# A decoder layer with 32 experts on one core: the split of an expert's fourth weight strip, ahead of the condition or behind it

## The chip, the cores and the metric

The kernel runs on one core of a Trainium2 chip. The core has TensorE (PE in the rows; its weight loads are PEld), VectorE (DVE), ScalarE (ACT), GpSimd (POOL) and SyncE (SP), which work at the same time and wait for one another through semaphores, and 16 DMA engines that all queues share. The metric is the device time of one execution in microseconds (us), lower is better. Three runs of the kernel before took 1853.65, 1854.08 and 1859.51 us; the median is 1854.08 us.

## What is computed

One decoder layer over 2048 tokens of width 1024, all in float32. A first sublayer mixes along the sequence (a state-space branch and a convolution branch, gates, an output projection, LayerNorm). The second sublayer is a mixture of 32 experts: each token goes to two experts of one group, and an expert's rows are worked off in blocks of 128:

```python
def expert_block(args):
    idx, e = args
    xb = xt[idx]
    hid = jax.nn.silu(xb @ w_gate[e]) * (xb @ w_up[e])
    return hid @ w_down[e]
```

The weighted results are summed back to their tokens, and a last LayerNorm follows. `w_gate[e]` and `w_up[e]` are 1024 x 256, `w_down[e]` is 256 x 1024. 4096 assignments over 32 experts make 128 rows an expert on average, so that an expert has one block of rows, or two, or three; the kernel reads the counts at run time.

## The kernel before

The change lies in the loop over the experts (`for e in range(NE)`, lines 1520 to 1552), which is written out 32 times. Order on each engine is the order in which the code is written; an engine works its queue off in that order, and an instruction that waits holds up all that is behind it.

**Weights.** An expert's weights come in as float32 and are split into a high part (a copy rounded to a shorter format, by ACT) and a low part (what is left, a subtraction by DVE), so that three matmuls with the short format stand for one in float32. The raw weights lie in `RAW[i]` (rows: `eraw`) for gate and up, side by side, and in `RD` (`erd`) for down; the split ones in `GU[i]` (`egu`) and `DN[i]` (`edn`). There are two sets, `i` = 0 and 1, for even and odd experts. Gate-and-up is cut into four strips, k = 0 to 3, of 256 rows each, and down into two, k = 4 and 5. `high(i, k)` is the copy on ACT (L1245), `low(i, k)` the subtraction on DVE, `step(i, k)` one after the other. The subtraction of a strip also sets its part of `RAW` free: `load(e, i)` has four DMAs on SP's queue, two (gate and up, L1223 and L1224) for strips 0 and 1 and two for strips 2 and 3, each of 512 KB; `load2` has one of 1 MB for down (L1229).

**A pass for expert e** (j = e % 2) does the matmuls of e, and splits the weights of e + 1 beside it:

1. POOL gathers the rows of the next expert into `XN` and, in conditions on the count (L1527), those of the second and third block of e into `X1` and `X2` (rows: `xhi`, `xlo`).
2. `step(1 - j, 0, 1, 2)` and `high(1 - j, 3)`: three strips of e + 1, and the copy of the fourth.
3. `block(e, 0, j)`: `gateup`, 24 matmuls of 128x512 into `pg`, three for each of 8 pieces of 128 rows of the weights, then `act`: SiLU on ACT and the product on DVE (`hid`).
4. `low(1 - j, 3)`, and `load(e + 3, 1 - j)`.
5. `turn(XN[j])`: 8 transposes of the next expert's rows on PE into `pt`, then the high part by ACT and the low part by DVE into the one tile `B` (`bhl`), which the next `gateup` reads. The third matmul of a `gateup` is the first that reads a low part of `bhl`.
6. `down(1 - j)`: 12 matmuls into `pd`, the down projection of the previous expert's last block.
7. `further(e, 1)`: a condition on the count (L1486). Where the expert has a second block, its body turns `hid` (`turnh`, 2 transposes into `ph`), emits the block before (`emit_last`: two copies of `pd` into `yy` by ACT, scaled by `ll`, with the split of `ph` into `hh` and `hl` in between, and a scatter with addition into `acc` by POOL, L1465), and does the second block with `gateup`, `act`, `turn(X1)` and `down`; a third block is nested in it. Else the body is `turnh` alone.
8. `emit(LQ ...)`: the same emission with the factor `lq`, of whichever block is due, with the split of `ph` (`hh` on ACT, L1447, `hl` on DVE) in between.
9. The two strips of down, k = 4 and 5, and `load2(e + 3, 1 - j)`.

Items 2, 4 and 9 stand only for `more`, that is for e = 1 to 30. PE, ACT, DVE and POOL all take the branch of L1486; SP has no condition there. `yy` has two buffers.

The lines of items 2 to 5 in the loop:

```python
        if more:
            step(1 - j, 0, 1, 2)
            high(1 - j, 3)
        block(e, 0, j, GU[j])
        if more:
            low(1 - j, 3)
            if e + 3 < NE:
                load(e + 3, 1 - j)
        turn(XN[j])
```

Of the kernel before, what the change touches and what calls it, by code (L numbers as in the profile page):

```python
# [26 lines left out]
NE = 32  # L27
# [58 lines left out]
def layer(ctx, tc, a, out, dbg=None):  # L86
# [17 lines left out]
    def bigt(shape, dt, name):  # L104
        n = 1
        for d in shape[1:]:
            n *= d
        return big.tile(shape, dt, name=name, tag="big", bufs=NBIG)
# [1107 lines left out]
    def rows(w, e):  # L1216
        return (w[e] if isinstance(e, int) else w[ds(e, 1)][0]).rearrange("(k p) f -> p k f", p=128)

    def load(e, i, halves=(0, 1)):
        if RAW[i] is None:  # L1220
            RAW[i] = bigt([128, 8, 512], F32, f"eraw{i}")
        for h in halves:
            SP.dma_start(RAW[i][:, 4 * h:4 * h + 4, 0:256], rows(wg, e)[:, 4 * h:4 * h + 4])  # L1223
            SP.dma_start(RAW[i][:, 4 * h:4 * h + 4, 256:512], rows(wu, e)[:, 4 * h:4 * h + 4])  # L1224

    def load2(e, i, q=SP):
        if not RD:
            RD.append(bigt([128, 2, 2, D], F32, "erd"))
        q.dma_start(RD[0][:, i], rows(wd, e))  # L1229


    def parts(i, k):
        if k < 4:
            if GU[i][k // 2] is None:
                GU[i][k // 2] = bigt([128, 2, 4, 512], F32R, f"egu{i}{k // 2}")
            t, r = GU[i][k // 2], k % 2
            return t[:, 0, 2 * r:2 * r + 2, :], t[:, 1, 2 * r:2 * r + 2, :], RAW[i][:, 2 * k:2 * k + 2, :]
        if DN[i] is None:
            DN[i] = bigt([128, 2, 2, D], F32R, f"edn{i}")
        return DN[i][:, 0, k - 4, :], DN[i][:, 1, k - 4, :], RD[0][:, i, k - 4, :]  # L1240

    def high(i, *ks):
        for k in ks:
            h, l, src = parts(i, k)
            A.activation(h, src, AF.Copy)  # L1245

    def low(i, *ks):
        for k in ks:
            h, l, src = parts(i, k)
            V.tensor_tensor(l, src, h.bitcast(F32), op=OP.subtract)  # L1250

    def step(i, *ks):
        for k in ks:
            high(i, k)
            low(i, k)
# [153 lines left out]
    def table(e):  # L1409
        CNT[e] = nc.values_load(cnt[0:1, e:e + 1], engines=ENG, min_val=0, max_val=S)  # L1410

    def gather(xb, idx):
        G.indirect_dma_start(out=xb, out_offset=None, in_=hd,
                             in_offset=bass.IndirectOffsetOnAxis(ap=idx, axis=0),
                             bounds_check=S - 1, oob_is_err=False)
# [6 lines left out]
    def turn(xb):  # L1422
        for b in range(2):
            for k in range(4):
                PE.transpose(PT[b][:, k, :], xb[:, (4 * b + k) * 128:(4 * b + k + 1) * 128], ident)
            hi = B[:, 4 * b:4 * b + 4, 0]
            A.activation(hi, PT[b], AF.Copy)
            V.tensor_tensor(B[:, 4 * b:4 * b + 4, 1], PT[b], hi.bitcast(F32), op=OP.subtract)
# [13 lines left out]
    def turnh():  # L1442
        for k in range(2):
            PE.transpose(PH[:, k, :], HID[:, 128 * k:128 * k + 128], ident)

    def splith():
        A.activation(HH, PH, AF.Copy)  # L1447
        V.tensor_tensor(HL, PH, HH.bitcast(F32), op=OP.subtract)

    def down(j):  # L1450
        dn = DN[j]
        for h in range(2):
            c = slice(512 * h, 512 * h + 512)
            for k in range(2):
                PE.matmul(PD[h], HH[:, k, :], dn[:, 0, k, c], start=k == 0, stop=False)
                PE.matmul(PD[h], HH[:, k, :], dn[:, 1, k, c], start=False, stop=False)
                PE.matmul(PD[h], HL[:, k, :], dn[:, 0, k, c], start=False, stop=k == 1)

    def emit(idx, factor, between=None):
        y = ep.tile([128, D], F32, name="yy", bufs=2)  # L1460
        for h in range(2):
            A.activation(y[:, 512 * h:512 * h + 512], PD[h], AF.Copy, scale=factor.bitcast(F32))  # L1462
            if not h and between:
                between()
        G.indirect_dma_start(out=acc, out_offset=bass.IndirectOffsetOnAxis(ap=idx, axis=0),  # L1465
                             in_=y, in_offset=None, bounds_check=S - 1, oob_is_err=False, compute_op=OP.add)

    def emit_last(e, between=None):
        emit(LL[:, e, 0:1], LL[:, e, 1:2], between)

    def block(e, b, i, gu):

        gateup(i, gu)
        act(i)

    def further(e, b):


        j = e % 2

        def end(b):
            turnh()
            if b > 1 and not e:
                emit(TAB[:, e, b - 2, 0:1], TAB[:, e, b - 2, 1:2])

        with tc.If(CNT[e] > 128 * b) as c:  # L1486
            end(b)
            if b > 1 and e:
                emit(TAB[:, e, b - 2, 0:1], TAB[:, e, b - 2, 1:2], splith)
            elif b == 1 and e:  # L1490
                emit_last(e - 1, splith)
            else:
                splith()
            block(e, b, (e + b) % 2, GU[j])
            if e + 1 < NE or b + 1 < JB:
                turn(XB[b])
            down(j)
            if b + 1 < JB:
                further(e, b + 1)
            else:  # L1500
                end(b + 1)
        with c.Else():
            end(b)
# [16 lines left out]
    for e in range(NE):  # L1520
        j = e % 2
        more = 0 < e < NE - 1
        if e + 2 < NE:
            table(e + 2)
        if e + 1 < NE:
            gather(XN[1 - j], NX[:, e + 1, 0:1])
        with tc.If(CNT[e] > 128):  # L1527
            gather(X1, NX[:, e, 1:2])
            if JB > 2:
                with tc.If(CNT[e] > 256):  # L1530
                    gather(X2, NX[:, e, 2:3])
        if more:
            step(1 - j, 0, 1, 2)
            high(1 - j, 3)
        block(e, 0, j, GU[j])
        if more:
            low(1 - j, 3)
            if e + 3 < NE:
                load(e + 3, 1 - j)
        turn(XN[j])  # L1540
        if e:
            down(1 - j)
        further(e, 1)
        if e:
            emit(LQ[:, e, 0:1], LQ[:, e, 1:2], splith)
        else:
            splith()
        if more:
            high(1 - j, 4, 5)
            low(1 - j, 4, 5)  # L1550
            if e + 3 < NE:
                load2(e + 3, 1 - j)
# [162 lines left out]
```

## Time and profile before

| what | value |
|---|---|
| median of three runs | 1854.08 us |
| the profiled execution, its own time | 1854.43 us |
| its span, first to last instruction | 1852.7 us |
| mean granted TensorE clock | 0.968 of full speed |
| TensorE busy with matmuls | 1703.9 us (92%) |
| VectorE busy | 1317.4 us (71%) |
| ScalarE busy | 692.4 us (37%) |

The span holds 1852.7 us of the execution's 1854.43 us; 1.7 us lie around it. A timeline row gives start and length in us, engine, line, operation, tiles (out<-in), shape and count; a bracket behind it is the time that the engine stood idle before it, and what it had waited for. L66 is the line of a helper through which all PE and DVE instructions go, so these are told apart by their tiles. "DVEq" is DVE's sequencer, here at the branch of L1486. The matmuls of a group overlap: the 24 of a `gateup` follow one another every 0.23 us, though a single one is shown with some 0.4 us.

### The profile page before, as it was taken

The numbers are of one execution on the slowest core, as the hardware profiler recorded it, in microseconds if no ns is written. First come the engines' busy times: TensorE is split into PE (matmuls) and PEld (weight loads), VectorE is DVE, ScalarE is ACT, GpSimd is POOL, SyncE is SP. The second block draws the span as 40 slices with busy tenths as digits, with TensorE's granted clock in tenths as the row PEclk, the third lists the DMA queues.
The fourth block names the chain that finished last, engine by engine and source line by source line (L and its number), as shares of the span: only waits on it lengthen the run. The fifth ranks groups of instructions, "written<-read, shape, count | busy, mean of one in ns | idle before, by whom it ended". The sixth has DMA issues, their size and how long they took to land. (4 is left out here: it accounts for less than half of the span.)

```text
span 1852.7 us, 23925 instructions
## 1 busy us (share of the span) xinstructions
PE 1703.9 (92%) x8368; PEld 1371.0 (74%) x8369; DVE 1317.4 (71%) x2429; ACT 692.4 (37%) x1069; POOL 312.6 (17%) x319
## 2 busy tenths in 40 slices
PE   8999999999999999999999999973999999999930
PEld 7888877777777778777888888862777787777730
DVE  5798787777876874766576778885675556657648
ACT  5111221222222222633321122324675556666744
POOL 2000001101110101000000012212343233333315
PEclk9999999999999999999999999986999999999975
DMA  6321432432342336333463423546988878789755
GB/s 215 95 92 46 119 78 71 145 98 77 100 149 70 101 99 222 109 122 114 172 191 119 148 92 115 182 164 197 304 266 256 253 211 253 230 261 327 223 176 231
DMA packets 214027, 300.81 MB, mean 162 GB/s; under 512 B 29391, under 2 KB 159521, under 8 KB 211313
## 3 DMA queue, kind: packets, MB, share of 16 engines
q1 hardware_dynamic: 166496, 213.32, 35.0%
q0 software_dynamic: 23152, 56.06, 11.6%
q10 hardware_dynamic: 24224, 29.47, 4.8%
q8 instruction: 86, 1.41, 0.3%
q14 instruction: 69, 0.56, 0.1%
HBM read 224.77 MB, written 92.31 MB: 171 GB/s over the span
## 5 line engine op out<-in xcount | busy, mean ns | idle before, releaser
L66 PE MATMUL mm<-xh,whi 128*128 128x512 f32 x896 | 360.8, 403 | 0.0
L66 PE MATMUL mm<-xl,whi 128*128 128x512 f32 x896 | 353.6, 395 | 0.0
L66 PE MATMUL mm<-xh,wlo 128*128 128x512 f32 x896 | 352.1, 393 | 0.0
L66 PE MATMUL pg<-egu,bhl 128*128 128x512 f32 x1176 | 287.4, 399 | 25.1 <-DVEq L1486 20.7
L66 DVE SCALAR_TENSOR_TENSOR cvw<-cvw,cw 128x1024 f32<-128x1024 f32 x240 | 292.1, 1280 | 0.0
L66 PEld LDWEIGHTS pg<-egu,bhl 128*128 128x128 f32 x1176 | 217.9, 189 | 78.1 <-issue 14.2
L66 PEld LDWEIGHTS mm<-xh,whi 128*128 128x128 f32 x896 | 168.3, 188 | 47.9 <-ACT y L712 5.8
L66 PEld LDWEIGHTS mm<-xh,wlo 128*128 128x128 f32 x896 | 168.2, 188 | 41.6
L66 PEld LDWEIGHTS mm<-xl,whi 128*128 128x128 f32 x896 | 168.6, 188 | 36.5 <-DVE xl L66 0.3
L66 PE MATMUL mm<-yt,whi 128*128 128x512 f32 x512 | 163.7, 401 | 2.0 <-ACT yt L858 1.5
L66 PE MATMUL mm<-wo,mh 128*128 128x512 f32 x512 | 162.5, 398 | 0.0
L66 DVE TENSOR_TENSOR egu<-eraw,egu 128x1024 fp32r<-128x1024 f32 x128 | 150.7, 1218 | 6.0 <-ACT egu L1245 5.9
L731 ACT ACTIVATE gt<-mm,cols 128x512 f32<-128x512 f32 x64 | 44.0, 688 | 265.4 <-PE mm L66 254.4
L66 PE MATMUL pd<-edn,hh 128*128 128x512 f32 x392 | 126.7, 404 | 1.0 <-ACT hh L1447 1.0
L1245 ACT ACTIVATE egu<-eraw 128x1024 fp32r<-128x1024 f32 x128 | 124.9, 1056 | 3.3 <-DMA td<-r_sd,r_sl 3.1
L66 PEld LDWEIGHTS mm<-yt,whi 128*128 128x128 f32 x512 | 96.6, 190 | 25.8 <-ACT yt L858 1.5
L66 PEld LDWEIGHTS mm<-wo,mh 128*128 128x128 f32 x512 | 94.2, 188 | 21.5 <-issue 1.2
L66 PE MATMUL mm<-yt,wlo 128*128 128x512 f32 x256 | 101.5, 396 | 0.0
L66 PE MATMUL mm<-wo,ml 128*128 128x512 f32 x256 | 101.0, 394 | 0.0
L66 DVE TENSOR_TENSOR edn<-erd,edn 128x1024 fp32r<-128x1024 f32 x64 | 75.7, 1225 | 33.0 <-ACT edn L1245 33.0
L1206 POOL DMA_INDIRECT td<-r_sd,r_sl x32 | 38.2, 1194 | 310.3 <-DVE r_sl L66 300.9
L1465 POOL DMA_INDIRECT acc<-yy,lq x31 | 49.2, 1589 | 244.8 <-ACT yy L1462 244.8
(300 smaller groups left out, 2561.3 us busy)
## 6 DMA issues: line engine op xcount, KB each, us to landing
eraw<-in_w_gate_dram SPq DMA_DIRECT2D x64, 512.0 KB
eraw<-in_w_up_dram SPq DMA_DIRECT2D x64, 512.0 KB
erd<-in_w_down_dram SPq DMA_DIRECT2D x32, 1024.0 KB
gd<-gt ACTq DMA_DIRECT2D x64, 256.0 KB
gl<-gd SPq DMA_DIRECT2D x64, 256.0 KB
wraw<-in_w_in_dram SPq DMA_DIRECT2D x28, 512.0 KB
xt<-in_x_dram SPq DMA_DIRECT2D x16, 512.0 KB
rg<-in_x_dram SPq DMA_DIRECT2D x8, 1024.0 KB
```

Of the source, the lines that this page charges most:

```text
L66: return f(*args, **kw)
L731: A.activation(gt, p, AF.Sigmoid, bias=cols[:, BI + 12 + m:BI + 13 + m])
L1206: d = G.indirect_dma_start(out=td, out_offset=bass.IndirectOffsetOnAxis(ap=sl[:, t, k:k + 1], axis=0), in_=sd[:, t, k, :], in_offset=None)
L1245: A.activation(h, src, AF.Copy)
L1465: G.indirect_dma_start(out=acc, out_offset=bass.IndirectOffsetOnAxis(ap=idx, axis=0), in_=y, in_offset=None, bounds_check=S - 1, oob_is_er ...
```

## The change

The copy and the subtraction of strip 3 go together, as `step(1 - j, 3)`, behind `further(e, 1)`, and `load(e + 3, 1 - j)` goes with them. No instruction is added or taken away.

```diff
         if more:
             step(1 - j, 0, 1, 2)
-            high(1 - j, 3)
         block(e, 0, j, GU[j])
-        if more:
-            low(1 - j, 3)
-            if e + 3 < NE:
-                load(e + 3, 1 - j)
         turn(XN[j])
         if e:
             down(1 - j)
         further(e, 1)
+        if more:
+            step(1 - j, 3)
+            if e + 3 < NE:
+                load(e + 3, 1 - j)
         if e:
             emit(LQ[:, e, 0:1], LQ[:, e, 1:2], splith)
         else:
```

On DVE, in the pass for e = 30, from the subtraction of strip 2 to the condition (`egu_10191` is the half of `GU` that holds strips 2 and 3, `eraw_9798` the raw tile), before:

```order
L66 TENSOR_TENSOR egu_10191<-eraw_9798,egu_10191 128x1024
L66 TENSOR_TENSOR hid<-hid,pg_10176 128x256
L66 TENSOR_TENSOR egu_10191<-eraw_9798,egu_10191 128x1024
L66 TENSOR_TENSOR bhl<-pt_10180,bhl 128x4x128
L66 TENSOR_TENSOR bhl<-pt_10181,bhl 128x4x128
L1486 COMPARE_AND_BRANCH
```

The same stretch now:

```order
L66 TENSOR_TENSOR egu_10191<-eraw_9798,egu_10191 128x1024
L66 TENSOR_TENSOR hid<-hid,pg_10176 128x256
L66 TENSOR_TENSOR bhl<-pt_10180,bhl 128x4x128
L66 TENSOR_TENSOR bhl<-pt_10181,bhl 128x4x128
L1486 COMPARE_AND_BRANCH
```

The second `egu_10191`, strip 3, has left the place between the product and the two subtractions of the turned rows.

On DVE, at the end of the condition of the same pass, before:

```order
L66 TENSOR_TENSOR bhl<-pt_10180,bhl 128x4x128
L66 TENSOR_TENSOR bhl<-pt_10181,bhl 128x4x128
L1486 UNCONDITIONAL_BRANCH x3
L66 TENSOR_TENSOR hl<-ph,hh 128x256
L66 TENSOR_TENSOR edn_10194<-erd,edn_10194 128x1024 x2
```

and now:

```order
L66 TENSOR_TENSOR bhl<-pt_10180,bhl 128x4x128
L66 TENSOR_TENSOR bhl<-pt_10181,bhl 128x4x128
L1486 UNCONDITIONAL_BRANCH x3
L66 TENSOR_TENSOR egu_10191<-eraw_9798,egu_10191 128x1024
L66 TENSOR_TENSOR hl<-ph,hh 128x256
L66 TENSOR_TENSOR edn_10194<-erd,edn_10194 128x1024 x2
```

Strip 3 now stands first behind the condition, ahead of the low part of the turned hidden block. On ACT its copy moves in the same way, from ahead of the SiLU to ahead of the first `yy` copy of `emit(LQ ...)`.

On SP's queue, one pass before:

```order
L1229 DMA erd<-in_w_down_dram 128x2x1024
L1223 DMA eraw_9798<-in_w_gate_dram 128x4x256
L1224 DMA eraw_9798<-in_w_up_dram 128x4x256
L1223 DMA eraw_9798<-in_w_gate_dram 128x4x256
L1224 DMA eraw_9798<-in_w_up_dram 128x4x256
L1486 UNCONDITIONAL_BRANCH
L1527 UNCONDITIONAL_BRANCH
```

and now:

```order
L1229 DMA erd<-in_w_down_dram 128x2x1024
L1223 DMA eraw_9798<-in_w_gate_dram 128x4x256
L1224 DMA eraw_9798<-in_w_up_dram 128x4x256
L1486 UNCONDITIONAL_BRANCH
L1223 DMA eraw_9798<-in_w_gate_dram 128x4x256
L1224 DMA eraw_9798<-in_w_up_dram 128x4x256
L1527 UNCONDITIONAL_BRANCH
```

The two loads for strips 0 and 1 keep their place; the two for strips 2 and 3, which wait for the subtraction of strip 3, move behind SP's jump over the condition. The order of the five loads among themselves is as before.

## Rows read from the trace of the kernel before

**Rows 1.** The page's second part, the span in 40 slices of 46.3 us: the busy tenths of PE, and the busy share of the DMA engines.

```profile
PE   8999999999999999999999999973999999999930
...
DMA  6321432432342336333463423546988878789755
```

**Rows 2.** One window over the loop over the experts. Columns: stretch, us, busy time and count of PE, PEld, DVE, ACT and POOL, granted TensorE clock, DMA share, GB/s.

```profile
1281.00:1772.00 491.00, 464.44 (x2224) 375.73 (x2223) 304.79 (x374) 312.73 (x469) 164.52 (x94) 0.99 0.82 248
```

**Rows 3.** The waits in that window, those of PE's matmuls for `pg`: who, for what, us in total, times, longest.

```profile
PE pg L66 <- DVEq L1486: 20.7, 15, 2.0
...
PE pg L66 <- DVE bhl L66: 4.2, 6, 0.8
```

**Rows 4.** The timeline over an expert with one block, from one `hh` to the next, PE, ACT and DVE.

```profile
1684.08 0.38 ACT L1447 ACTIVATE hh<-ph 128x256 fp32r<-128x256 f32 x1 [0.21 <-DVEq L1486]
1684.11 5.75 PE L66 MATMUL pg<-egu,bhl 128*128 128x512 f32 x24 [0.91 <-DVEq L1486]
...
1686.02 2.36 DVE L66 TENSOR_TENSOR edn<-erd,edn 128x1024 fp32r<-128x1024 f32 x2 [1.10 <-ACT edn L1245]
...
1691.71 0.42 DVE L66 TENSOR_TENSOR hid<-hid,pg 128x256 f32<-128x256 f32 x1
...
1692.04 1.22 DVE L66 TENSOR_TENSOR egu<-eraw,egu 128x1024 fp32r<-128x1024 f32 x1
...
1693.17 1.28 DVE L66 TENSOR_TENSOR bhl<-pt,bhl 128x512 fp32r<-128x512 f32 x2
...
1693.37 0.38 PE L66 MATMUL ph<-ident,hid 128*128 128x128 f32 x2
1693.72 0.69 ACT L1462 ACTIVATE yy<-pd,lq 128x512 f32<-128x512 f32 x1 [1.75 <-PE ph L66]
...
1694.63 0.39 ACT L1447 ACTIVATE hh<-ph 128x256 fp32r<-128x256 f32 x1 [0.21 <-DVEq L1486]
1694.66 2.58 PE L66 MATMUL pg<-egu,bhl 128*128 128x512 f32 x10 [0.91 <-DVEq L1486]
...
1695.05 0.42 DVE L66 TENSOR_TENSOR hl<-ph,hh 128x256 fp32r<-128x256 f32 x1 [0.59 <-ACT hh L1447]
```

**Rows 5.** The timeline over an expert with two blocks, which follows one with two blocks.

```profile
1403.38 0.38 ACT L1447 ACTIVATE hh<-ph 128x256 fp32r<-128x256 f32 x1
...
1408.92 1.92 POOL L1413 DMA_INDIRECT xhi<-hd,nx  x1 [0.30 <-issue]
...
1411.00 0.42 DVE L66 TENSOR_TENSOR hid<-hid,pg 128x256 f32<-128x256 f32 x1
...
1411.47 0.44 PE L66 MATMUL ph<-ident,hid 128*128 128x128 f32 x2 [0.35 <-DVE hid L66]
...
1412.00 0.38 ACT L1447 ACTIVATE hh<-ph 128x256 fp32r<-128x256 f32 x1 [0.15 <-ACT yy L1462]
...
1412.47 1.28 DVE L66 TENSOR_TENSOR bhl<-pt,bhl 128x512 fp32r<-128x512 f32 x2
...
1413.21 5.32 PE L66 MATMUL pg<-egu,bhl 128*128 128x512 f32 x22 [0.84 <-DVE bhl L66]
1413.24 1.61 POOL L1465 DMA_INDIRECT acc<-yy,ll  x1 [2.39 <-ACT yy L1462]
...
1418.36 1.03 PE L66 MATMUL pt<-ident,xhi 128*128 128x128 f32 x8
...
1422.00 0.38 PE L66 MATMUL ph<-ident,hid 128*128 128x128 f32 x2
...
1422.14 5.81 PE L66 MATMUL pg<-egu,bhl 128*128 128x512 f32 x24
1422.82 0.69 ACT L1462 ACTIVATE yy<-pd,lq 128x512 f32<-128x512 f32 x1 [2.69 <-DMA acc<-yy,ll]
1423.41 0.38 ACT L1447 ACTIVATE hh<-ph 128x256 fp32r<-128x256 f32 x1
```

**Rows 6.** SP's issues in the timeline of that expert: the load for down, and the two for strips 2 and 3.

```profile
1407.71 0.37 SPq L1229 DMA_DIRECT2D erd<-in_w_down_dram  x1
...
1412.62 0.37 SPq L1223 DMA_DIRECT2D eraw<-in_w_gate_dram  x1
1413.04 1.61 SPq L1224 DMA_DIRECT2D eraw<-in_w_up_dram  x1
```

**Rows 7.** POOL's DMAs in the window of rows 2: count, and median us from issue to landing.

```profile
acc<-yy,lq POOLq DMA_INDIRECT x30, 6.4
xhi<-hd,nx POOLq DMA_INDIRECT x29, 8.8
...
acc<-yy,ll POOLq DMA_INDIRECT x14, 8.8
acc<-yy,tab POOLq DMA_INDIRECT x3, 6.2
```

**Rows 8.** Windows over two experts with one block each, one behind the other (columns as in rows 2).

```profile
1674.77:1685.32 10.55, 9.64 (x47) 7.78 (x46) 8.86 (x10) 8.58 (x13) 3.69 (x3) 1.00 1.05 360
1685.32:1695.87 10.55, 9.64 (x47) 7.79 (x46) 8.86 (x10) 8.59 (x13) 3.70 (x3) 1.00 1.07 330
```

**Rows 9.** All instructions of the tile `xhi` over the whole span: the time to landing of its gathers.

```profile
DMA to landing us min/median/max: 4.1/8.7/10.0
```

## Prediction

> **What bounds the kernel now.** I read the slices first: PE is at nine tenths nearly throughout, and the DMA engines, at two to four tenths in the first half, are at eight or nine in the stretch that the change touches [rows 1]. So PE is the engine to watch and DMA the one that could get in the way. Next the window over the loop over the experts: of 491.00 us PE is busy 464.44, at a granted clock of 0.99, which is the upper of its two levels; 26.6 us are idle [rows 2]. No reordering on ACT and DVE can bring more than these 26.6 us, for PE's work stays as it is. Then the waits: of that idle time 20.7 us are 15 waits of a `gateup` for DVE's sequencer at the branch, and 4.2 us are 6 waits for `bhl` [rows 3]. Both are waits for the queue in which the subtraction of strip 3 stands, just ahead of the two subtractions of the turned rows.
>
> The passes have to be told apart. In the loop POOL issues 30 `lq` scatters, one a pass, 14 `ll` (a second block) and 3 `tab` (a third) [rows 7]. So passes 1 to 30, the ones that split weights, are 16 with one block, 11 with two and 3 with three.
>
> **One block: three loops.** Such a pass takes 10.55 us, from `hh` at 1684.08 to `hh` at 1694.63 [rows 4]. What is to be seen: `hh` and the next `gateup` start together, both released by DVE's sequencer, 0.18 and 0.21 us after the second `bhl` subtraction ends (1693.17 + 1.28 = 1694.45). The loop that binds is therefore on ACT and DVE: from `hh` over the copies and subtractions of five strips to `hid`, 7.63 us (1691.71 - 1684.08), 0.33 to the next slot (1692.04), 1.13 for strip 3 (to 1693.17), 1.28 for `bhl`, 0.18 to `hh`: 10.55. PE waits 0.91 us in each.
>
> The change takes the 1.13 out of this loop: 9.42 us. Two other loops stand behind it. PE alone: `gateup` at 1684.11 to `ph` at 1693.37 is 9.26, and the next `gateup` follows `ph` by 0.14 where nothing holds it (1422.00 to 1422.14) [rows 4, 5]: 9.40. And a mixed one: from `gateup` 9.26 to `ph`, 0.35 to the first `yy` copy (1693.72), 0.59 from there to `hh` (1422.82 to 1423.41), so 10.20; from `hh` 9.24 to the end of `bhl` without strip 3 (7.63 + 0.33 + 1.28) and 0.21 to a `gateup`, which is the one after the next, so 9.45. That is 19.65 for two experts, 9.83 each [rows 4, 5]. The slowest of the three sets the pace: 9.83 instead of 10.55, **0.72 us less in each of 16 passes, 11.5 us**.
>
> **Where strip 3 goes.** I cost its new place at nothing, by these covers. On ACT its copy (1.05 us) lands ahead of the `yy` copy, where ACT stands idle for 1.75 us waiting for `ph`; were that gone, the 1.05 would go straight into the mixed loop, 0.5 us a pass. On DVE the subtraction (1.13) falls between `bhl` and `hl`, where 0.59 are idle; `hl` starts some 0.5 us later and ends ahead of the subtraction of strip 4, which waits 1.10 us for its copy anyway [rows 4]. PE reads strip 3 from the 19th of the 24 matmuls on, 18 x 0.23 = 4.2 us after the start of `gateup`, and strip 3 is done about 1.3 us after that start; the margin is some 2.9 us. ACT's copy also leaves the place ahead of the SiLU; that brings nothing by itself, since `hid` waits for DVE's subtractions.
>
> **Two and three blocks.** Here the second `gateup` waits inside the condition for the first `bhl` subtraction (0.84 us at 1413.21), and strip 3 stands ahead of that subtraction (`hid` ends at 1411.42, `bhl` starts at 1412.47) [rows 5]. Taken alone this would bring 0.84. But another loop passes through this expert and doesn't hold strip 3: `hh` at 1403.38 to the `ll` scatter at 1413.24 is 9.86; its landing frees the `yy` buffer for which the `lq` copy at 1422.82 waits, 9.58 after the issue; 0.59 to `hh`: 20.03 us [rows 5]. It is unchanged but for the landing. With the median landing of 8.8 [rows 7] and the same 0.1 behind it the loop is 19.35. PE's floor for two blocks is 2 x 9.40 = 18.80, reached with a landing of 8.25 or less. A third bound is the gather into `X1`, issued at 1408.92; with its median of 8.8 it is there at 1417.72, and the transposes that now start at 1418.36 could start by some 0.5 us sooner, not by the 0.98 that strip 3 took [rows 5, 7]. So each of the 14 passes gains between nothing (landings as in rows 5, or longer) and 20.03 - 18.80 = 1.23 us. I take 0.4, near the lower end, since both transfers bind in part: **14 x 0.4 = 5.6 us**.
>
> The landing is not independent of the change. The two loads of strips 2 and 3 are now issued at 1412.62 and 1413.04, right ahead of the scatter [rows 6]; afterwards they are issued behind the condition, at about 1422, so the `ll` scatter and the gather into `X1` share the engines with 2 MB of loads of this pass instead of 3 MB, and the `lq` scatter and the gathers of the next pass, which now land in 6.4 and 8.8 [rows 7], get the other 1 MB beside them. That a scatter lands sooner without loads beside it the rows bear out: `lq` and `tab` at 6.4 and 6.2 in the median against 8.8 for `ll` [rows 7]. The Trainium skill states the mechanism ("DMA: Bandwidth & Descriptors", section "Queues, rings and completion order"): each DMA engine takes its queues in turn, a packet at a time, so a scatter beside queued loads gets only its turn. By the page alone `ll` would land like `lq` now, in 6.4 us, and the two-block passes would come down to PE's floor: 14 x 1.23 = 17.2 us instead of 5.6. I don't go so far, because the `X1` gather is issued before the loads in question in either kernel and still has 2 MB beside it.
>
> **Sum.** 11.5 + 5.6 = 17.1 us off the profiled execution's own 1854.43 us (span 1852.7): 1837.3 us. The median of the runs shown is 1854.08, 0.35 below, so the forecast is 1837 us, 0.9% less.
>
> **Rivals.** *PE's floor.* All waits of rows 3 go, 20.7 + 4.2 = 24.9 us: 1829.5 us. It needs the landings to shorten and the mixed loop not to bind. For it: the loads that leave. Against: the mixed loop holds in every run of one-block passes.
>
> *DMA becomes the bound of one-block passes.* Two of them, one behind the other, show a DMA share of 1.05 and 1.07 at 360 and 330 GB/s [rows 8]; that is 3.80 and 3.48 MB, 3.64 in the mean, and at 360, the most that I see over a pass, 3.64 MB take 10.1 us, not 9.83. Then each saves 0.45, 7.2 us in all, and the two-block passes nothing: 1847 us. Against it: loads are issued two passes ahead of their use, about 20 us, and a run of one-block passes would have to be long to use that up. The Trainium skill gives a limit that speaks against the change here ("DMA: Bandwidth & Descriptors", section "Specifications"): about 358 GB/s from memory for a core. The rows agree in so far as no pass shows more than 360.
>
> *The wait stays.* A `gateup` waits for a count of DVE's work, and strip 3 now stands just behind the branch. If the first matmul waits for strip 3 too, the 1.13 us stay in the one-block loop, only in another place: 10.55 again, and what is left is the two-block passes' 0 to 5.6 us: 1849 to 1854 us. The wait in the rows is for DVE's sequencer at the branch itself, which stays ahead of strip 3; this speaks against.
>
> *Slower: the gather into `X1` comes too late.* The delayed 1 MB now runs beside the `lq` scatter and the gathers of the next pass. The transposes start 9.44 us after the gather's issue (1418.36 - 1408.92) [rows 5], so from a landing of about 9.34 on, each of 14 passes gets longer, and from 11.5 / 14 = 0.82 beyond that, 10.16, the kernel is slower than before. The longest gather into `xhi` took 10.0 [rows 9]. At 11 us the price is 14 x 1.66 = 23.2, less 11.5: 11.7 us, 1866 us.
>
> **How the numbers follow.** About 0.3%, 5.6 us here, is what a measurement of this kernel can tell from no change: faster is below 1848.5. The forecast, with landings between the ends (1832 to 1843), has 0.55; PE's floor 0.14; DMA as the bound 0.13, all still faster; the wait that stays 0.11, no difference to be measured; the late gather 0.07, slower. Faster 0.82, same 0.11, slower 0.07. The range goes from PE's floor, 1829, to just over the DMA case, 1849; it leaves out most of the last two cases, 0.16 in all.
>
> **What would show it.** Right: the `gateup` waits for DVE's sequencer fall from 20.7 us to under 8; one-block passes last 9.4 to 10.3 us; `hid` is followed at once by `bhl`, and strip 3 by `hl` with no idle time on ACT ahead of `yy` to speak of; the waits for `bhl` inside the condition vanish; `ll` lands in less than 8.8 us. Wrong: a `gateup` that starts only after strip 3; waits of PE for `xhi` or `xlo`; `yy` copies of `lq` that wait longer for `ll`; a copy of strip 0 or 2 that waits for its load.

## The result, and the profile after

The changed kernel takes 1838.88 us in the median of four runs (1836.41 to 1839.48); the kernel before, run beside it, takes 1856.01 (1853.65 to 1859.51). The ratio is 0.9904, with a 95% interval from 0.9883 to 0.9925: faster by about 17 us, 0.9%. The profiled execution of the changed kernel took 1839.48 us, span 1837.8; the forecast was 1837.

The slices of the page look as before [rows 1]: PE and the DMA engines.

```profile
PE   8999999999999999999999999992999999999930
...
DMA  7321432432342335343464333447788968889855
```

What changed shows in the window over the loop over the experts (columns as in rows 2):

```profile
1281.00:1757.00 476.00, 463.33 (x2227) 376.96 (x2228) 307.44 (x374) 317.44 (x469) 164.44 (x94) 0.99 0.83 256
```

PE is busy as long as before within 1.1 us, but idle for 12.7 us instead of 26.6 [rows 2]. The waits in the same window say what is left: who, for what, us in total, times, longest.

```profile
ACT yy L1462 <- PE ph L66: 16.1, 19, 1.1
ACT yy L1462 <- DMA acc<-yy,ll: 14.2, 8, 2.8
...
PE pg L66 <- DVEq L1486: 6.7, 10, 1.2
...
PE ph L66 <- DVE hid L66: 3.3, 5, 1.4
```

The waits of `gateup` for DVE's branch fell from 20.7 to 6.7 us, and those for `bhl` are gone [rows 3]. What stayed is ACT's wait for the landing of the `ll` scatter: 14.2 us here, 17.1 before.

The 30 `lq` scatters mark the passes. POOL's timeline shows the first and the last:

```profile
1303.18 1.65 POOL L1465 DMA_INDIRECT acc<-yy,lq  x1 [11.88 <-ACT yy L1462]
...
1753.09 1.59 POOL L1465 DMA_INDIRECT acc<-yy,lq  x1 [5.44 <-ACT yy L1462]
```

From first to last are 449.9 us, against 465.7 in the trace of before: 15.8 less. The first comes 1.4 later, which accounts for most of the difference to the 14.95 us between the two profiled executions. With the 29 distances between these marks sorted by the blocks of the expert at whose scatter they end (the first pass has no mark at its start):

| us | 15 with one block | 11 with two | 3 with three |
|---|---|---|---|
| before | 159.7 | 220.4 | 85.6 |
| after | 147.4 | 217.3 | 85.2 |

**One block**, the timeline of PE, ACT, DVE, to be held against [rows 4]:

```profile
1662.70 5.80 PE L66 MATMUL pg<-egu,bhl 128*128 128x512 f32 x24 [0.19 <-DVEq L1486]
1663.08 0.38 ACT L1447 ACTIVATE hh<-ph 128x256 fp32r<-128x256 f32 x1
...
1670.70 0.41 DVE L66 TENSOR_TENSOR hid<-hid,pg 128x256 f32<-128x256 f32 x1
...
1671.03 1.28 DVE L66 TENSOR_TENSOR bhl<-pt,bhl 128x512 fp32r<-128x512 f32 x2
...
1671.97 0.38 PE L66 MATMUL ph<-ident,hid 128*128 128x128 f32 x2
1672.33 0.69 ACT L1462 ACTIVATE yy<-pd,lq 128x512 f32<-128x512 f32 x1 [1.04 <-PE ph L66]
1672.45 1.22 DVE L66 TENSOR_TENSOR egu<-eraw,egu 128x1024 fp32r<-128x1024 f32 x1
...
1672.51 5.74 PE L66 MATMUL pg<-egu,bhl 128*128 128x512 f32 x24 [0.16 <-DVEq L1486]
1672.91 0.38 ACT L1447 ACTIVATE hh<-ph 128x256 fp32r<-128x256 f32 x1
...
1673.60 0.42 DVE L66 TENSOR_TENSOR hl<-ph,hh 128x256 fp32r<-128x256 f32 x1
```

To be seen: `bhl` follows `hid` at once. The next `gateup` starts at 1672.51, 0.20 after `bhl` ends, while strip 3 (1672.45) is still at work: it does not wait for strip 3. From `gateup` to `gateup` are 9.81 us. `hh` and `gateup` no longer start together: `hh` comes 0.94 behind `ph`, ruled by the `yy` copy.

**Two blocks**, the expert of [rows 5], in the same places:

```profile
1402.52 0.38 ACT L1447 ACTIVATE hh<-ph 128x256 fp32r<-128x256 f32 x1
...
1410.60 0.44 PE L66 MATMUL ph<-ident,hid 128*128 128x128 f32 x2
1410.79 5.76 PE L66 MATMUL pg<-egu,bhl 128*128 128x512 f32 x24
...
1412.36 1.61 POOL L1465 DMA_INDIRECT acc<-yy,ll  x1 [2.39 <-ACT yy L1462]
...
1420.87 0.69 ACT L1462 ACTIVATE yy<-pd,lq 128x512 f32<-128x512 f32 x1 [1.27 <-DMA acc<-yy,ll]
1420.88 0.37 SPq L1223 DMA_DIRECT2D eraw<-in_w_gate_dram  x1
1421.30 0.50 SPq L1224 DMA_DIRECT2D eraw<-in_w_up_dram  x1
1421.46 0.38 ACT L1447 ACTIVATE hh<-ph 128x256 fp32r<-128x256 f32 x1
```

The second `gateup` follows `ph` without a wait. From `hh` to the `ll` scatter are 9.84 (9.86 before), from there to the `lq` copy 8.51 (9.58 before), and 0.59 to `hh`: 18.94 instead of 20.03. The loop is the old one; in this pass only the landing in it got shorter. The two loads of strips 2 and 3 (1420.88 and 1421.30) are behind it now.

### The profile page after: what moved, and what is told of

It is laid out like the page before. It is cut to its first block, busy times and chain, and to the rows that moved or that the text cites. A ratio compares the mean times of both kernels' runs of the same rounds, so it can differ in the third digit from the quotient of the medians.

```text
span 1837.8 us, 23924 instructions
## 1 busy us (share of the span) xinstructions
PE 1702.5 (93%) x8368; PEld 1370.4 (75%) x8369; DVE 1319.6 (72%) x2429; ACT 696.7 (38%) x1069; POOL 312.7 (17%) x319
## 5 line engine op out<-in xcount | busy, mean ns | idle before, releaser
L66 DVE TENSOR_TENSOR egu<-eraw,egu 128x1024 fp32r<-128x1024 f32 x128 | 150.8, 1219 | 15.1 <-ACT egu L1245 12.7
```

The lines of the kernel that those rows point to most:

```text
L66: return f(*args, **kw)
```

## The experiments

Theory: `gateup` and `hh` were held by DVE's branch, and strip 3 stood ahead of it; behind the branch it lies in idle time. Two-block passes gain little, since the landing of `ll` holds them. The rivals: the buffer is the larger part; the gain comes from ACT's copy or from the loads; the new place only moves the cost. Each ratio is to the kernel before, run beside the one of its row. The last three columns are the sums of the table above, from scatter to scatter in the profiled execution.

| kernel | median us | ratio to before, 95% interval | one | two | three |
|---|---|---|---|---|---|
| behind_turn | 1860.02 | 1.0019 [1.0006, 1.0032] | 161.8 | 222.0 | 86.3 |
| yy3 | 1837.38 | 0.9899 [0.9880, 0.9917] | 151.0 | 211.2 | 84.6 |
| late_load | 1860.50 | 1.0019 [1.0008, 1.0031] | 161.4 | 222.3 | 87.5 |
| low_behind | 1838.88 | 0.9901 [0.9884, 0.9917] | 146.1 | 218.7 | 85.0 |
| hh_first | 1838.33 | 0.9903 [0.9879, 0.9927] | 151.2 | 213.0 | 86.1 |
| yy4 | 1830.46 | 0.9863 [0.9839, 0.9886] | 145.6 | 211.5 | 84.7 |
| before_yy4 | 1848.97 | 0.9963 [0.9948, 0.9977] | 158.4 | 215.5 | 85.9 |
| twice | 1845.17 | 0.9943 [0.9922, 0.9964] | 150.3 | 220.9 | 85.4 |
| behind_turn_yy4 | 1846.62 | 0.9951 [0.9933, 0.9968] | 159.0 | 213.4 | 85.5 |
| half_load | 1835.09 | 0.9884 [0.9863, 0.9906] | 146.1 | 215.4 | 84.7 |
| yy4_last | 1862.37 | 1.0036 [1.0021, 1.0050] | 153.1 | 228.7 | 93.7 |
| yy4_last_x1 | 1836.95 | 0.9897 [0.9879, 0.9914] | 161.2 | 212.7 | 84.6 |

### behind_turn: half the way, still ahead of the branch

```diff
             step(1 - j, 0, 1, 2)
-            high(1 - j, 3)
         block(e, 0, j, GU[j])
+        turn(XN[j])
         if more:
-            low(1 - j, 3)
+            step(1 - j, 3)
             if e + 3 < NE:
                 load(e + 3, 1 - j)
-        turn(XN[j])
```

> Strip 3 is split behind the subtractions of the turned rows, as in the change, but still ahead of the condition, as before. Theory (a one-block pass is held by DVE's arrival at the branch, so the place against the condition counts): one-block passes stay at 10.55 us with a wait of a gate-up for DVE's sequencer of about 0.9 to 1.7 us each, 20 us in all; only the waits for the turned rows inside the condition (4.2 us) go; 1850 to 1853 us. Rival (what counts is that the turned rows' low parts come first): one-block passes at 9.4 to 10.4 us as in the change, 1839 us.

One-block passes are at 10.54 as before, except for some in which the clock was low (below). One of them:

```profile
1687.60 1.28 DVE L66 TENSOR_TENSOR bhl<-pt,bhl 128x512 fp32r<-128x512 f32 x2
...
1688.80 1.22 DVE L66 TENSOR_TENSOR egu<-eraw,egu 128x1024 fp32r<-128x1024 f32 x1
...
1690.18 0.38 ACT L1447 ACTIVATE hh<-ph 128x256 fp32r<-128x256 f32 x1 [0.20 <-DVEq L1486]
...
1690.22 5.75 PE L66 MATMUL pg<-egu,bhl 128*128 128x512 f32 x24 [0.90 <-DVEq L1486]
```

`bhl` ends at 1688.88, but `gateup` starts 1.34 later, 0.20 behind the end of strip 3 (1690.02). So it is not the place of strip 3 against `bhl` that counts for these passes, but against the branch. The waits of PE and ACT in its loop, from 1303 us on:

```profile
PE pg L66 <- DVEq L1486: 17.6, 12, 2.0
PE ph L66 <- DVE hid L66: 7.2, 8, 2.8
```

```profile
ACT yy L1462 <- DMA acc<-yy,ll: 31.7, 9, 5.5
```

The waits for `bhl` are gone, but the two-block passes did not get shorter: what the trace shows in their place is a longer wait for `ll` (31.7 us instead of 17.1). The gain that was expected of them did not come: 1860.02 us, not 1850 to 1853. Why the kernel is 0.2% slower than before is not shown; in the loop of its profiled execution the clock falls to its lower level in three places, in that of before in one.

### late_load: only the loads

In the kernel before, the loads of strips 2 and 3 go behind the load for down.

```diff
-                load(e + 3, 1 - j)
+                load(e + 3, 1 - j, (0,))
...
                 load2(e + 3, 1 - j)
+                load(e + 3, 1 - j, (1,))
```

> The kernel before, with only the two loads of strips 2 and 3 moved, behind the load for down, so that they are issued some 5 us into the next pass instead of right ahead of the ll scatter. Theory (the ll scatter lands late because these loads stand beside it): ll lands in 6.5 to 8 us instead of 8.8, the waits for it shrink from 17.1 us to under 8, two-block passes lose 0.2 to 0.5 us each, one-block passes stay at 10.55; 1850 to 1853 us. Rival (the landing is set by the gathers ahead of it in POOL's own queue): nothing moves, 1854 to 1856 us.

Nothing is gained: 1860.50 us, ratio 1.0019, outside what I and the rival expected; here, too, the profiled execution has three places at the lower clock. The waits for `ll` fell only from 17.1 to 14.5 us, and strip 3, still in its place, held the passes. The loads alone are not the cause.

### low_behind: ACT's copy stays, DVE's subtraction moves

```diff
             step(1 - j, 0, 1, 2)
+            high(1 - j, 3)
...
-            step(1 - j, 3)
+            low(1 - j, 3)
```

> The change, but with ACT's copy of strip 3 left ahead of the block, where it was; only the subtraction and the loads go behind the condition. Theory (only DVE's queue counts, the SiLU has slack because the product waits for DVE): the same time as the change, 1837 to 1840 us, waits for DVE's sequencer under 8 us. Rival (the copy ahead of the SiLU delays the copies of the turned rows on ACT): the turned rows come up to 1 us later, 1845 to 1852 us.

The same time as the changed kernel (that the medians agree to a hundredth of a microsecond is chance). The gain hangs on DVE's subtraction; where ACT does its copy makes no difference. The waits of the `yy` copies for `ll` come to 27.1 us in this trace, against 14.2 in that of the changed kernel, at the same time: the total of these waits in one trace says little by itself.

### twice: what the new place hides

```diff
             step(1 - j, 3)
+            low(1 - j, 3)
```

> The changed kernel with the subtraction of strip 3 done twice over, one behind the other, behind the condition; the second writes the same values again. It measures what the new place hides. My theory: the first fits into the 0.59 us of idle time ahead of hl and the 1.10 ahead of the subtraction of strip 4; the second adds 1.13 us of DVE work of which some tenths are still covered, so that each of 30 passes gets 0.4 to 0.8 us longer where ACT and DVE bind and less where PE or a scatter does: 8 to 20 us in all, 1847 to 1859 us. Rival 1: the new place hides any DVE work, no change, 1838 to 1841 us. Rival 2: the place hides nothing: 30 x 1.13 = 34 us, 1873 us.

The 29 marked passes became 6.7 us longer in all (456.6 from first to last mark instead of 449.9), where 30 x 1.13 = 34 us of work were added: a little under what was expected (1845.17 us, not 1847 to 1859), and neither rival. The timeline of a one-block pass, from strip 3 to the strips of down:

```profile
1665.76 2.48 DVE L66 TENSOR_TENSOR egu<-eraw,egu 128x1024 fp32r<-128x1024 f32 x2
1665.81 5.79 PE L66 MATMUL pg<-egu,bhl 128*128 128x512 f32 x24 [0.19 <-DVEq L1486]
...
1668.16 0.41 DVE L66 TENSOR_TENSOR hl<-ph,hh 128x256 fp32r<-128x256 f32 x1
...
1668.49 2.35 DVE L66 TENSOR_TENSOR edn<-erd,edn 128x1024 fp32r<-128x1024 f32 x2
```

Both subtractions take 2.48, and DVE has no idle time left up to `edn`; in the changed kernel it waits 0.81 there. The cover of the first subtraction is real, and the second has used it up.

### yy3, yy4 and before_yy4: the buffer

```diff
-        y = ep.tile([128, D], F32, name="yy", bufs=2)
+        y = ep.tile([128, D], F32, name="yy", bufs=3)
```

> The change with three buffers for the emitted rows (yy) instead of two, so that the copy with factor lq doesn't wait for the landing of the scatter with factor ll of the same pass. Theory (two-block passes are held by that landing): the waits for acc<-yy,ll (14.2 us, 8) go, two-block passes fall from 19.6 us in the mean to 18.9 to 19.3, 1831 to 1835 us. Rival (the gather into X1 or the DMA engines hold them): the wait moves to the transposes of xhi or to a later one, two-block passes stay at 19.6 and the time at 1838 to 1840 us.

The two-block passes fall from 217.3 to 211.2 us, as they should if the landing of `ll` held them. The one-block passes rise, though, from 147.4 to 151.0: the code has three emissions a pass, so that with three buffers `lq` always gets the buffer of the `lq` before, and its copies wait for that scatter (10.8 us in 6 waits). So the total, 1837.38 us, missed 1831 to 1835. With `bufs=4`:

> The changed kernel with four yy buffers instead of two. My theory: the two-block passes are held by the ll scatter, whose landing frees the buffer that the lq copy of the same pass waits for; with three buffers that wait went in two-block passes (4.5 us in all) but came up for the lq scatter of the pass before in one-block passes. With four no copy waits for a scatter of its own pass or of the one before: one-block passes stay at 147 us in all, two-block passes fall from 217 to about 211 us, 1831 to 1835 us. Rival: the gather into X1 or the DMA engines hold these passes as soon as the buffer does not: 1836 to 1840 us, with waits of PE for xhi.

This is the fastest version, 1830.46 us, a little under the range expected. The window over its loop, and its waits from 1303 us on:

```profile
1281.00:1748.00 467.00, 459.40 (x2221) 375.69 (x2221) 307.48 (x374) 316.99 (x469) 162.75 (x94) 1.00 0.84 261
```

```profile
PE pg L66 <- DVEq L1486: 3.2, 7, 0.6
PE pg L66 <- ACT yy L1462: 2.3, 3, 0.8
...
PE pt L66 <- DMA xhi<-hd,nx: 0.6, 1, 0.6
```

PE stands idle for 7.6 us of 467, and the gather into `X1` makes it wait for 0.6 us in all: neither it nor the DMA engines hold these passes. The same edit in the kernel before:

> The kernel before with four yy buffers, strip 3 where it was. My theory: one-block passes keep 10.55 us, since their loop (copies and subtractions up to the second bhl subtraction, then the branch) holds no scatter; two-block passes lose the wait for the ll landing but keep strip 3 ahead of the first bhl subtraction, so they gain some tenths each, 2 to 6 us in all: 1850 to 1855 us. Rival: the buffer is the larger part of what the change brought, and passes of all kinds gain: below 1846 us.

1848.97 us, a little under the lower end. One-block passes keep 10.55; two-block passes are all at 19.5 to 19.65, where strip 3 ahead of `bhl` holds them. So the two edits are separate: the move brings 12.8 us in one-block passes with four buffers (158.4 to 145.6) and 4.0 in two-block passes (215.5 to 211.5, 0.36 each).

### behind_turn_yy4: the two-block term by itself

The edit of behind_turn, with `bufs=4`.

> The kernel before with four yy buffers, and with the split and the loads of strip 3 moved only half the way: behind the two subtractions of the turned rows and still ahead of the condition. It isolates the two-block term from the scatter that held those passes with two buffers. My theory: the first bhl subtraction no longer stands behind strip 3, so the two-block passes lose their 0.7 us loop and come down from 19.6 (four buffers, strip 3 at its old place) to about 19.2, 211 to 213 us in all; the one-block passes still find strip 3 ahead of DVE's branch and keep 10.55, 158 us in all: 1844 to 1847 us. Rival: the one-block passes gain as well, since what counts is strip 3 ahead of bhl and not ahead of the branch: 1830 to 1836 us.

Both sums are about where they were expected: one-block passes unchanged, two-block passes at 213.4, 2.1 us shorter than with strip 3 at its old place. That is half of what yy4 shows; one wait of 1.9 us ahead of the transposes, which the trace puts down to issue, is in it, and what caused that wait is open.

### half_load: without the loads of strips 2 and 3

```diff
-                load(e + 3, 1 - j)
+                load(e + 3, 1 - j, (0,))
```

> The changed kernel without the loads of strips 2 and 3 in the loop, which leaves out 1 MB of weights a pass; experts from the fourth on are computed with strips of earlier ones, by the same instructions. It tests what the prediction says of the landings. My theory: with 2 MB of loads beside it instead of 3 the ll scatter lands in less than 8 us, the waits of yy for ll (14 us in all) fall to under 6, and the two- and three-block passes get shorter by 0.4 to 0.7 us each; one-block passes keep their pace, since no transfer is in their loop: 1829 to 1834 us. Rival: the scatter's landing does not depend on the loads: 1837 to 1841 us and the same waits for ll.

1835.09 us, between the two. POOL's scatter in its loop, with the median time to landing:

```profile
acc<-yy,ll POOLq DMA_INDIRECT x14, 8.2
```

8.2 against 8.8 in the kernel before [rows 7]; the trace of the changed kernel gives no median for these scatters. yy4, which has all the loads, shows 8.1, hh_first 8.3, and the two kernels with strip 3 and its loads ahead of the condition (before_yy4, behind_turn_yy4) 8.6. So the landing gets shorter by about half a microsecond when these loads leave the condition, and not further when they are not made at all. The waits for `ll` fall to 12.1 us, not under 6.

### hh_first: the mixed loop

```diff
-            emit(LQ[:, e, 0:1], LQ[:, e, 1:2], splith)
+            splith()
+            emit(LQ[:, e, 0:1], LQ[:, e, 1:2])
```

> The changed kernel with the split of the turned hidden block (hh on ACT, hl on DVE) put ahead of the two yy copies of emit(LQ ...) instead of between them. My theory: in the changed kernel the one-block passes are held by the mixed loop, gateup to ph to the first yy copy to hh to the next gateup but one, and its 0.59 us between the start of the yy copy and hh then count once in two passes, less what hh still waits for ph (some 0.1). One-block passes then fall from about 9.83 in the mean to about 9.55, 15 x 0.25 = 3 to 5 us in all, 1834 to 1836 us. Rival: another loop (PE alone, 9.40, or ACT and DVE) binds already, or the later yy copies delay the scatter and with it the buffer that the next passes wait for: no change, 1838 to 1841 us, with more idle time of ACT ahead of yy.

My expectation missed, and the rival's number came: no change in the total, and one-block passes settled at 9.98, longer than the 9.83 of the changed kernel. Its timeline shows why:

```profile
1680.82 0.38 ACT L1447 ACTIVATE hh<-ph 128x256 fp32r<-128x256 f32 x1 [1.29 <-DVEq L1486]
...
1681.10 1.26 ACT L1462 ACTIVATE yy<-pd,lq 128x512 f32<-128x512 f32 x2
...
1682.23 2.02 ACT L1245 ACTIVATE edn<-erd 128x1024 fp32r<-128x1024 f32 x2
...
1689.35 1.28 DVE L66 TENSOR_TENSOR bhl<-pt,bhl 128x512 fp32r<-128x512 f32 x2
...
1690.83 0.38 ACT L1447 ACTIVATE hh<-ph 128x256 fp32r<-128x256 f32 x1 [0.96 <-PE ph L66]
```

Between `hh` and the copies of down there are now both `yy` copies instead of one. That is the loop on ACT and DVE, 9.42 in the prediction, with another 0.57 (1.26 - 0.69) in it: 9.99, and `hh` again waits for DVE's branch (1.29 us at 1680.82). I had looked at the mixed loop alone, and put its gain into the loop beside it. The two-block passes are shorter (213.0), since the copy that waits for `ll` no longer holds up `hh` (these waits are 2.6 us instead of 14.2); the two cancel.

### yy4_last and yy4_last_x1: both `yy` copies behind the copies of down

```diff
-        if e:
-            emit(LQ[:, e, 0:1], LQ[:, e, 1:2], splith)
-        else:
-            splith()
+        splith()
         if more:
             high(1 - j, 4, 5)
             low(1 - j, 4, 5)
+        if e:
+            emit(LQ[:, e, 0:1], LQ[:, e, 1:2])
+        if more:
             if e + 3 < NE:
                 load2(e + 3, 1 - j)
```

> The changed kernel with four yy buffers, and with hh and hl and the two strips of down ahead of both yy copies of emit(LQ ...). My theory: with the yy copies ahead of hh the mixed loop (gateup, ph, yy, hh) held one-block passes at 9.8; with hh ahead of both but the copies of down behind them, ACT and DVE's loop grew by the second yy copy and held them at 9.99. Here neither yy copy is in a loop, so that one-block passes fall to PE's own 9.40 to 9.45, 142 us in all instead of 145.6, and waits of pg for DVE's branch vanish: 1826 to 1829 us. Rival: the scatter and with it POOL's queue come some 1.6 us later, the gather into X1 lands late and PE waits for xhi in 14 passes: 1832 to 1845 us.

What the rival named came, and cost more than its 1832 to 1845: 1862.37 us, 0.4% slower than before. The one-block passes did not come down to 9.45 either; in the run of three they take 9.6 to 10.0 from `gateup` to `gateup`. PE's waits over the loop:

```profile
PE pt L66 <- issue: 11.8, 6, 4.6
PE pt L66 <- DMA xhi<-hd,nx: 11.3, 10, 3.0
```

Both are transposes that wait; in the changed kernel the two come to 0.9 us. This is the case that the prediction priced as "the gather into `X1` comes too late", brought about by another edit. To see whether that is the cause, the two gathers change places:

```diff
-        if e + 1 < NE:
-            gather(XN[1 - j], NX[:, e + 1, 0:1])
         with tc.If(CNT[e] > 128):
             gather(X1, NX[:, e, 1:2])
...
+        if e + 1 < NE:
+            gather(XN[1 - j], NX[:, e + 1, 0:1])
```

> The kernel that came out slower, four yy buffers and both yy copies behind the copies of down, with one more edit: POOL issues the gather into X1 (and X2) ahead of the gather into XN instead of behind it. It tells whether the lateness of the X1 gather is the cause of the loss. My theory: it is; the gather is then issued some 2.4 us sooner (one gather of POOL, 2.1, and 0.3 behind it), against the 1.6 us that the later scatter cost, so that the waits of PE for xhi, and those shown as issue ahead of the transposes, fall from 23 us to under 4, and the half-clock windows go: 1825 to 1831 us. Rival: the loss lies elsewhere, in the later yy copies (PE's waits for pd) or in ACT's order: above 1845 us.

It is, for the larger part: two-block passes fall from 228.7 to 212.7 us, three-block ones from 93.7 to 84.6, and the time to 1836.95. But PE's waits ahead of the transposes only halve, from 23.1 to 12.3 us, in a profiled execution that at 1845.92 was the longest of five. Four of them, 7.4 us in all, still stand behind a second `gateup`, where `X1` is turned; three, 3.7 us, are for `XN`. So the expected 1825 to 1831 was missed, and yy4 stays the best.

## Why the prediction was right

- **The bound.** PE's idle time was to be the ceiling, 26.6 us; 13.9 of it went.
- **One block, 16 x 0.72 = 11.5.** Over the 15 marked passes the kernel saved 12.3 us. One pass of before holds a stretch at the lower clock (11.82 instead of 10.55), so the saving by the change is about 11.0, 0.73 each. The mean is 9.83 as predicted, but in part by luck, for few passes take 9.83. Eight are at 9.4, most of them behind an expert with more blocks; four, each behind one of those, at 10.2 to 10.4; two in a longer run at 9.83 and 9.87; and one at 11.18. That one is a late mark: its scatter is issued at 1685.32, 1.65 behind the end of its `yy` copies, for a reason that the trace does not show, while the two `gateup`s there start 10.03 apart. What speaks for the mixed loop is that such neighbours add up to 19.6 to 19.8, against the 19.65 worked out for two, and that it reads as worked out: 9.27 to `ph`, 0.36 to `yy`, 0.58 to `hh` (1662.70 to 1672.91), then 9.23 and 0.20. behind_turn shows that the branch was the cause: ahead of it, 10.54; behind it, 9.8. Counted from `gateup` to `gateup` instead, the 16 one-block passes save 13.4 us and the 14 others 2.5: the split between the two terms hangs on the marks by about 1 us, their sum does not.
- **Two and three blocks, 14 x 0.4 = 5.6.** 3.5 us were saved, 0.25 each, with a stretch at the lower clock in one of them; without it (1.6 us) about 5.1, 0.36 each, the same as the 0.36 between before_yy4 and yy4. The step held: the loop over the landing of `ll` goes on as worked out, and with four buffers the floor near 18.8 appears: from `gateup` to `gateup`, 10 of the 11 two-block passes of yy4 take 18.77 to 18.88 us, in the trace of before 3 of 11.
- **The landing depends on the change.** Right in sign, by about half a microsecond (8.6 to 8.8 with these loads in the condition, 8.1 to 8.3 without). The Trainium skill's rule that each DMA engine takes its queues in turn ("DMA: Bandwidth & Descriptors", section "Queues, rings and completion order") fits the other side as well: in yy4 the `lq` scatter, which now has the loads beside it, lands in 7.4 instead of 6.3 in before_yy4; hh_first, which has them beside it as well, shows 6.5. But the 6.4 that I had worked out from it for `ll` does not come when these loads are left out: 8.2. In yy4_last and yy4_last_x1 `ll` does land in 6.5 and 6.7, with all loads made, and `lq` in 9.0 and 9.2. So more than these loads sets the landings; what else does is open.
- **Strip 3 at no cost.** Held: low_behind shows that ACT's part is free, twice that DVE has room for the first subtraction and for most of a second. (The margin for PE was 2.8 us, not 2.9: 18 x 0.23 is 4.1.)
- **A sign that I read wrongly.** I wrote that ACT would have no idle time ahead of `yy` to speak of. It has 1.04 to 1.09 a pass. ACT's work in a pass is the same, so its idle time of 1.75 falls only by the 0.72 that the pass loses.
- **The rivals.** PE's floor, 1829.5, needed another edit: yy4, 1830.46. The DMA engines as a bound: yy4 runs the same loads in 8 us less. The wait that stays: refuted by the start of `gateup` 0.06 behind that of strip 3. The late gather into `X1`: 0.4 us in one wait here, but yy4_last made it real.

The forecast was 1.9 us short of the measured median. Its base was the median of three runs of the kernel before, 1854.08; with the fourth it is 1856.01, and that is the 1.9. Measured against it the kernel saves 17.1 us, just the sum of the prediction. So close a hit is luck: other medians of the kernel before lie between 1855.28 and 1857.45, and the two profiled executions are 14.95 apart.

## What to carry to other kernels

In this kernel, an instruction ahead of a branch on one engine held up what the other engines waited for at that branch, though its result was needed only later: in behind_turn `gateup` starts 0.20 us behind strip 3, where the data it needs had been ready for 1.34. A piece of work that nobody needs ahead of a branch can go to the far side, if its engine is idle there. Before an order is changed, write down every loop through the engines with its length, also those that don't bind: here they were 10.55, 9.83 and 9.42, and moving work from one to the next (hh_first) or delaying what a third queue sends (yy4_last) gave the gain back. What brought the most after the move was a buffer: with four `yy` buffers both edits together bring 1.4%.

## What the runs showed of the hardware that I had not expected

Inside a loop that keeps PE busy for 97% of the time, the granted clock falls to the lower of its two levels, 1.2 instead of 2.4 GHz, for a short stretch just behind a short pause of PE. In the changed kernel, one such place, windows (columns as in rows 2) and PE's timeline:

```profile
1348.99:1352.40 3.41, 1.57 (x8) 0.90 (x7) 3.26 (x5) 2.77 (x5) 0.00 (x0) 1.00 0.90 320
1352.40:1355.80 3.40, 3.40 (x10) 2.63 (x9) 2.99 (x5) 3.40 (x4) 2.88 (x2) 0.50 1.06 360
```

```profile
1350.14 0.41 PE L66 MATMUL ph<-ident,hid 128*128 128x128 f32 x2 [0.79 <-DVE hid L66]
1351.60 7.33 PE L66 MATMUL pg<-egu,bhl 128*128 128x512 f32 x24 [1.05 <-DVEq L1486]
```

PE had stood idle for 0.79 and 1.05 us, with two transposes in between; then it worked without a pause at a granted clock of 0.50, and that `gateup` took 7.33 us where others take 5.75 to 5.8. So behind waits of under 2 us in all came another 1.6 us of loss. In the trace of yy4_last it came behind an idle time of 4.61 us:

```profile
1717.30:1720.70 3.40, 0.00 (x0) 0.00 (x0) 0.00 (x0) 0.00 (x0) 1.61 (x1) 1.00 0.52 170
1721.30:1724.70 3.40, 3.40 (x12) 2.82 (x11) 1.84 (x3) 2.25 (x3) 0.00 (x0) 0.50 0.34 75
```

The trace of before has one such place in the loop, those of behind_turn, late_load and yy4_last three or four each, yy4 none; its longest wait of PE between the first and the last `lq` scatter is 0.82. Not each pause has it: in yy4_last, waits of 2.49 and 1.12 us were followed by none, and before_yy4 has seven of 1.66 to 1.73 and no such place. What decides is left open, but where the clock did fall, some 2 us of waiting on PE cost nearly twice their own length.
